# Decoder layer on one core: decay columns loaded once, one product for the sample sums, and padded rows of the matmuls' moving operand

## The chip, the cores and the metric

The kernel runs on one core of one Trainium2 chip. The metric is the device time of one execution in microseconds (us). Before the change it is 2003.5 us, the median of three runs (2000.65 to 2004.73).

## What is computed

One inference step of one decoder layer (DEPTH is 1) for two groups of requests that share the weights: 256 prompt tokens, and 8 samples of one token each. All arrays are float32, D is 2048, the feed-forward width is 5504.

```
proj = x @ w_in                      # split into q, k, v, g, a_lr(16), cb, cc, ch, mq, z_a, z_b, z_m
log_a = log_sigmoid(a_lr @ w_gla_a2 + b_gla_a2) / 16
o, s_gla = gla_recurrence(q, k, v, log_a, s_gla)       # 4 heads, state 256 x 512 a head and sample
y_a = (rms_norm(o) * silu(g)) @ w_gla_out
y_b = (cb * causal_conv3(cc * ch)) @ w_conv_out
y_m = softmax(mq @ mem_k^T / 16) @ mem_v @ w_mem_out   # prompt: mem = mem_prompt @ w_mem_k, w_mem_v; samples: caches
m = (sigmoid(z_a)*y_a + sigmoid(z_b)*y_b + sigmoid(z_m)*y_m) @ w_o
x1 = layer_norm(2**0.25 * x + m)
f = (silu(causal_conv3(x1 @ w_ffn_gate) + b) * (x1 @ w_ffn_up)) @ w_ffn_down
y = layer_norm(2**0.25 * x1 + f)
```

Besides y, the memory's keys and values of the prompt and the new states (recurrence, convolution, feed-forward convolution) are written out.

## The kernel before

Everything is held transposed: 128 channels on the partitions, and a row of NT = 264 float32 (256 prompt tokens, 8 samples) for each block of 128 channels. A row of x is thus 1056 bytes, and the tiles XH and XL (L320, L321) hold the 16 rows of x one behind the other, so that row kt begins 1056·kt bytes into the tile. Float32 precision is made out of the faster fp32r matmul: x and every weight are split into a high part (rounded to fp32r) and a low part (the rest), and for each block of weights three matmuls are summed: weights high by x high (L302), weights high by x low (L303), weights low by x high (L304). X1H and X1L (L1155, L1156) hold the output of the first norm in the same way, in the place of XH and XL.

`group` (L280) computes 512 output channels. It walks over the 16 rows of x two at a time (a granule, L260): SP loads a 512 KB block of weights into one of four staging buffers `ws`, ScalarE rounds it to `wh` and VectorE subtracts for `wl` (both on L277, three buffers each), and TensorE runs 4 x 2 x 3 = 24 matmuls of 264 columns, for each of the 4 output blocks first the even row and then the odd one. After each granule `tick` (L229) advances a clock by one and works off what is due: `later(n, f)` runs f in n ticks, and a queue holds units that load something on SP and then work on it (`put`, `pop`). `flush` (L243) empties the queue and runs all that waits. Instructions of an engine run in the order in which a scheduler has put them; that order follows the program, moved by priorities.

The order of the stages: memory queries of x (L394); keys and values of the prompt's memory (L509), with the samples' key caches read meanwhile by `key_unit` (L425: a cache block, and a row of queries from DRAM spread over the partitions, `T<-dq`); attention into the memory (L548 to L577: product L554, maximum L557, L558, exponential L561, transpose L568, second product L575); `flush` at L578; the decay's projection (L591); q, k and v; the z_m, convolution, z_b, g and z_a projections with the output projections of the branches; w_o (L1118); the first norm; gate, up and down (L1204 on); the second norm.

The places that the change touches:

- **The decay's columns** (L591): the 32 columns from A0 of w_in (16 of the decay and 16 more) are wanted three times side by side, 96 columns, for the three products with w_gla_a2 split into high and low. They are loaded three times for each of two blocks of eight rows, six loads of 128 KB, and multiplied as a group of 96 columns, 16 rows x 3 = 48 matmuls. L593 and L594 make the high and the low part of the result.
- **The sums over partitions** (`sum_rows`, L459): six times (two for the memory's values of the samples, four for the heads' states) a tile R of 128 partitions x 8 samples x 16 is summed over the 4 partitions that are equal modulo 32. Four float32 matmuls of 32 columns add up into one place (L473), each with another 128-column window of `strip`, whose block of 32 columns holds the sum of four identities; VectorE copies the result out (L474).
- **A head's own key** (L635 to L640): two float32 matmuls of 8 columns (L638), one for each half of the 256 channels.
- **The memory's keys and values** (L528): four stores of 512 KB from the POOL queue, at once when a block is done.
- **The samples' past rows of the feed-forward convolution** (L1057 to L1059): one tile `fr` of 86 partitions x 8 x 128, of the S4 buffers that the samples' state units use too, is filled by two transfers of 172 KB from the POOL queue. `turn_fpast` transposes it in two halves, 20 and 24 ticks later (L1067).
- **Small tiles**: masks, vs, cpast, clast, omS, qkb, qas, and later fpast and flast, each have a place of their own.

Of the kernel before, what the change touches and what calls it, by code (L numbers as in the profile page):

```python
# [17 lines left out]
P = 128  # L18
# [16 lines left out]
def layer_kernel(ctx, tc, x_prompt, x_sample, mem_prompt, cache_mem_k, cache_mem_v, state_gla, state_conv,  # L35
# [15 lines left out]
    def big(dt=F32, shape=(P, 4, NT)):  # L51
        return sb.tile(list(shape), dt, tag="T4", bufs=16, name=nm("T4"))
# [13 lines left out]
    def small():  # L66
        return ps.tile([P, 512], F32, tag="sm", bufs=3, name=nm("sm"))
# [46 lines left out]
    smask = sb.tile([P, NP], F32, name="smask")  # L114
    masks = sb.tile([P, len(LEVELS) + 1, P], I8, name="masks")
    upper = masks[:, len(LEVELS)]
    strip = sb.tile([P, 7 * 32], F32, name="strip")
    vcol = sb.tile([P, NV], F32, name="vcol")
    fcol = sb.tile([P, 172], F32, name="fcol")

    quads = lambda c: strip[:, 96 - 32 * c:224 - 32 * c]
# [121 lines left out]
    def flush():  # L243
        while queue:
            pop()
        while waiting:
            due(True)
# [174 lines left out]
    pS = sb.tile([P, 2, 32], F32, tag="qs", name="pS")  # L422
    omS = sb.tile([P, 8, NS], F32, name="omS")

# [34 lines left out]
    def sum_rows(sums, b, z, dst, after=None):  # L459


        if b == 0:
            sums[0] = t2(F32, (P, NS, 16))
        zt = t2(F32, (P, 512))
        V.transpose(zt, z)
        R = sums[0]
        V.tensor_reduce(R[:, b], zt.rearrange("p (c j) -> p c j", j=32), AX.X, ALU.add)

        def product():
            pt = small()  # L470
            o = pt[:, 0:4 * NS].rearrange("p (b j) -> p b j", b=NS)
            for c in range(4):
                T.matmul(o, quads(c), R.rearrange("p b (j c) -> p b j c", c=4)[:, :, :, c], start=(c == 0), stop=(c == 3))  # L473
            V.tensor_copy(dst() if callable(dst) else dst, pt[:, 0:4 * NS].rearrange("p (b j) -> p j b", b=NS))  # L474
            if after:
                after()

        if b == NS - 1:
            later(3, product)
# [29 lines left out]
    for name, w, dst in (("k", w_mem_k[0], o_mk), ("v", w_mem_v[0], o_mv)):  # L509
# [18 lines left out]
        for m in range(2):  # L528
            G.dma_start(dst[0, 0, m * P:(m + 1) * P].rearrange("m h d -> m (h d)"), mt_[m])
        mtok[name] = mt_  # L530
# [17 lines left out]
    for c in range(2):  # L548
# [21 lines left out]
        for hh in range(2):  # L570
            for d in range(2):
# [13 lines left out]

    wr = big(F32, (96, 1024))
    wa2 = big(F32R, (96, 1024))
    G.memset(wr, 0.0)
    for i in range(3):
        G.dma_start(wr[32 * i:32 * i + 16], w_gla_a2[0])  # L590
# [7 lines left out]
    eas = sb.tile([P, H, 2, NS], F32, name="eas")  # L598
    vs = sb.tile([P, 4, H, NS], F32, name="vs")
# [3 lines left out]
    qkb = sb.tile([P, H, NS], F32, name="qkb")  # L603
    qas = sb.tile([P, H, 2, NS], F32, name="qas")

# [5 lines left out]
    def head(h, q, k, vf):  # L611
# [16 lines left out]
        def decays_of_samples():  # L628

            S.activation(eas[:, h], la[:, :, NP:NT], AF.Exp, scale=1.0 / 16.0)  # L630
            dot = tiny((P, 2, NS))
            V.tensor_mul(dot, qks[:, 0, h], qks[:, 1, h])
            later(1, lambda: (V.tensor_mul(qas[:, h], qks[:, 0, h], eas[:, h]), own_key(dot)))

        def own_key(dot):  # L635
            pz = small()
            for kt in range(2):
                T.matmul(pz[:, 0:NS], onesm, dot[:, kt], start=(kt == 0), stop=(kt == 1))  # L638
# [306 lines left out]

    cpast = sb.tile([P, 16, 8], F32, name="cpast")
    clast = sb.tile([P, 10, 8], F32, name="clast")
    cr = t2(F32, (P, P))
# [117 lines left out]

    later(20, lambda: turn_fpast(0))  # L1067
    later(24, lambda: turn_fpast(4))

# [332 lines left out]
```

## Time and profile before

| | |
|---|---|
| median of 3 runs | 2003.5 us (2000.65 to 2004.73) |
| the profiled execution | 2005.06 us |
| its span, first to last instruction | 2003.3 us |
| mean granted TensorE clock | 0.996 of full speed |
| TensorE busy | 1984.9 us (99%), 15,721 matmul records |
| VectorE, ScalarE, POOL busy | 1296.7, 986.3, 164.1 us |
| moved by DMA | 439 MB, 219 GB/s |

Each matmul record of the trace lasts longer than the distance to the next, since matmuls are pipelined: a record of 264 columns shows about 285 ns, and the next one begins about 122 ns after it. So busy time hides how fast TensorE goes; what counts is the distance from start to start. A float32 matmul appears as two records, an fp32r one as one. `[6.28 <-ACT wh L277]` behind a line is the idle time of that engine just before it and what is taken to have ended it.

### The profile page before, as it was taken

To read this page: it belongs to the slowest core of one execution; us is meant where nothing else is said; L and a number is where in the kernel's file an instruction comes from. 1 tells how busy PE (TensorE), PEld (TensorE's weight loads), DVE (VectorE), ACT (ScalarE), POOL (GpSimd) and SP (SyncE) were. 2 spreads that over 40 slices of the span, in tenths; PEclk is the share of its full clock that TensorE was granted. 3 is DMA by queue.
4 is the path that set the end of the run, shared out by engine and by line. 5 is a ranking of instruction groups with operands and counts; after the bars stand their busy time and mean duration, and the time that the engine had idled before them with its cause. 6 is when DMAs were issued, how large, how long until landed. Compare 5 with 4: busy or idle time off the path is not lost.

```text
span 2003.3 us, 38161 instructions
## 1 busy us (share of the span) xinstructions
PE 1984.9 (99%) x15721; PEld 1950.6 (97%) x15721; DVE 1296.7 (65%) x1947; ACT 986.3 (49%) x1348; POOL 164.1 (8%) x240
## 2 busy tenths in 40 slices
PE   9998999999999999999999999999999999999998
PEld 9887999999999999999999998999999999999997
DVE  5675866566676867865444787666665556666655
ACT  4433654454554555554444346555554445555533
POOL 4000030021310211100000201000000000000100
PEclk9999999999999999999999999999999999999999
DMA  8895866566666667866555567877777787777753
GB/s 282 272 316 189 274 201 198 176 211 197 189 190 195 201 190 241 259 173 183 179 179 181 178 213 252 256 236 231 233 246 249 259 254 238 232 233 247 237 177 119
DMA packets 235199, 439.00 MB, mean 219 GB/s; under 512 B 22862, under 2 KB 29571, under 8 KB 234889
## 3 DMA queue, kind: packets, MB, share of 16 engines
q1 hardware_dynamic: 229120, 426.86, 68.9%
q0 software_dynamic: 5040, 8.79, 1.3%
q8 instruction: 123, 2.02, 0.4%
q10 hardware_dynamic: 864, 0.92, 0.1%
q14 instruction: 52, 0.42, 0.1%
HBM read 409.76 MB, written 26.90 MB: 218 GB/s over the span
## 4 chain that ended last, share of the span: by engine, by line
PE 72%; DVE 1%; ACT 0%; issue 0%; DVEq 0%; ACTq 0%
PE mm L303 23%; PE mm L302 23%; PE mm L304 23%; PE sm L803 1%; PE sm L679 0%; PE sm L781 0%; DVE G L935 0%; PE sm L473 0%; PE sm L1276 0%; DVE wl L277 0%; PE sm L849 0%; PE sm L783 0%; PE bank L1331 0%; PE mm L1139 0%; ACT wh L277 0%
## 5 line engine op out<-in xcount | busy, mean ns | idle before, releaser
L277 DVE TENSOR_TENSOR wl<-ws,wh 128x1024 fp32r<-128x1024 f32 (+2 forms) x651 | 802.6, 1234 | 582.0 <-ACT wh L277 580.2
L277 ACT CAST wh<-ws 128x1024 fp32r<-128x1024 f32 (+2 forms) x651 | 676.1, 1039 | 878.0 <-PE mm L303 770.0
L302 PE MATMUL mm<-XH,wh 128*128 128x264 f32 (+1 forms) x2064 | 592.8, 287 | 1.8 <-ACT wh L277 1.0
L303 PE MATMUL mm<-XL,wh 128*128 128x264 f32 (+1 forms) x2064 | 588.8, 286 | 0.0
L304 PE MATMUL mm<-XH,wl 128*128 128x264 f32 (+1 forms) x2064 | 586.2, 285 | 0.7 <-DVE wl L277 0.7
L302 PE MATMUL mm<-T,wh 128*128 128x264 f32 x1456 | 415.1, 285 | 0.0
L303 PE MATMUL mm<-T,wh 128*128 128x264 f32 x1456 | 414.2, 284 | 0.0
L304 PE MATMUL mm<-T,wl 128*128 128x264 f32 x1456 | 413.8, 284 | 0.0
L302 PEld LDWEIGHTS mm<-XH,wh 128*128 128x128 f32 (+1 forms) x2064 | 390.0, 189 | 2.7 <-ACT wh L277 1.2
L302 PE MATMUL mm<-X1H,wh 128*128 128x264 f32 x1376 | 391.5, 284 | 0.0
L303 PE MATMUL mm<-X1L,wh 128*128 128x264 f32 x1376 | 391.1, 284 | 0.0
L304 PE MATMUL mm<-X1H,wl 128*128 128x264 f32 x1376 | 391.0, 284 | 0.0
L303 PEld LDWEIGHTS mm<-XL,wh 128*128 128x128 f32 (+1 forms) x2064 | 389.4, 189 | 0.5 <-DVE XL L317 0.2
L304 PEld LDWEIGHTS mm<-XH,wl 128*128 128x128 f32 (+1 forms) x2064 | 387.8, 188 | 1.2 <-DVE wl L277 1.0
L302 PEld LDWEIGHTS mm<-T,wh 128*128 128x128 f32 x1456 | 274.1, 188 | 0.1
L303 PEld LDWEIGHTS mm<-T,wh 128*128 128x128 f32 x1456 | 274.0, 188 | 0.1
L304 PEld LDWEIGHTS mm<-T,wl 128*128 128x128 f32 x1456 | 273.8, 188 | 0.0
L302 PEld LDWEIGHTS mm<-X1H,wh 128*128 128x128 f32 x1376 | 259.4, 189 | 0.2 <-issue 0.2
L303 PEld LDWEIGHTS mm<-X1L,wh 128*128 128x128 f32 x1376 | 259.0, 188 | 0.2 <-DVE T L1160 0.2
L304 PEld LDWEIGHTS mm<-X1H,wl 128*128 128x128 f32 x1376 | 258.4, 188 | 0.0
L1080 POOL DMA_DIRECT2D out_dram<-S x2 | 1.1, 551 | 637.2 <-DVE S L1077 637.2
L521 PE MATMUL mm<-wl,T 128*128 128x512 f32 x128 | 50.6, 395 | 0.0
(363 smaller groups left out, 1485.7 us busy)
## 6 DMA issues: line engine op xcount, KB each, us to landing
ws<-in_w_in_dram SPq DMA_DIRECT2D x255, 512.0 KB, 4.0
ws<-in_w_ffn_down_dram SPq DMA_DIRECT2D x84, 512.0 KB, 4.8
ws<-in_w_ffn_gate_dram SPq DMA_DIRECT2D x80, 512.0 KB, 4.4
ws<-in_w_ffn_up_dram SPq DMA_DIRECT2D x80, 512.0 KB, 4.7
S<-in_state_gla_dram SPq DMA_DIRECT2D x64, 512.0 KB, 5.3
ws<-in_w_gla_out_dram SPq DMA_DIRECT2D x32, 512.0 KB, 3.7
ws<-in_w_o_dram SPq DMA_DIRECT2D x32, 512.0 KB, 4.2
out_dram<-S SPq DMA_DIRECT2D x32, 512.0 KB, 4.2
```

The costliest lines, as they stand in the source:

```text
L277: split_at[:] = [S.copy(wh, st).ins, V.tensor_sub(wl, st, wh.bitcast(F32)).ins]
L302: T.matmul(p, wh[:, t, cs], xh(kt), start=(kt == 0), stop=False)
L303: T.matmul(p, wh[:, t, cs], xl(kt), start=False, stop=False)
L304: i = T.matmul(p, wl[:, t, cs], xh(kt), start=False, stop=(kt == nk - 1))
L521: T.matmul(pts[m], a, wl[:, t], start=False, stop=False)
L803: T.matmul(pt, kd[:, st, kt * P:(kt + 1) * P], vt[:, st], start=(st == 0), stop=(st == 1))
L1080: G.dma_start(o_pffn[0, 0, u].rearrange("(k f) -> k f", f=P), rows[:, 0])
```

## The change

The decay's 32 columns are loaded once for each block of eight rows. ScalarE spreads them into three copies of the high part, VectorE puts the low part beside them, which makes 128 weight columns; two matmuls a row (all 128 columns by x high, 96 by x low) take the place of three, and the low products come out in a fourth block of 32 partitions, which a fourth copy of w_gla_a2 takes in.

The sums over partitions become one float32 matmul of 128 columns with `modulo` (four identities of 32 added, four times side by side), whose result is copied out in four pieces of 32 partitions, by VectorE and ScalarE in turn. A head's own key adds its two halves on VectorE first and needs one matmul.

Rows of XH, XL, X1H and X1L are 288 elements apart instead of 264, 1152 bytes, of which 264 are used. The room comes from one tile `part`: masks, vs, cpast, clast, omS, qkb and qas lie in `early`, and fpast and flast in `late`, which takes the same place after it.

The stores of the memory's keys and values are put 2 and 8 ticks later, and the queue alone is emptied behind the attention, not all that waits. The feed-forward past is loaded on SP, two pieces of 43 rows for each sample and one sample a tick, and turned 14 and 18 ticks later.

```diff
-    masks = sb.tile([P, len(LEVELS) + 1, P], I8, name="masks")
+    early = sb.tile([P, 1150], F32, tag="part", name="early")
+    masks = early[:, 0:256].bitcast(I8).rearrange("p (l t) -> p l t", t=P)
+    vs = early[:, 256:384].rearrange("p (j h b) -> p j h b", j=4, h=H)
+    cpast = early[:, 384:512].rearrange("p (b k) -> p b k", k=8)
+    clast = early[:, 512:592].rearrange("p (t j) -> p t j", j=8)
+    omS = early[:, 592:656].rearrange("p (d b) -> p d b", b=NS)
+    qkb = early[:, 656:688].rearrange("p (h b) -> p h b", b=NS)
+    qas = early[:, 688:752].rearrange("p (h k b) -> p h k b", h=H, k=2)
...
-        G.memset(strip, 0.0)
-        for a in range(4):
-            G.tensor_tensor(strip[:, 96:128], strip[:, 96:128], ident[:, 32 * a:32 * a + 32], ALU.add)
+        i4 = ident.rearrange("p (a i) -> p a i", a=4)
+        V.tensor_add(modulo[:, 0:2], i4[:, 0:2], i4[:, 2:4])
+        V.tensor_add(modulo[:, 3], modulo[:, 0], modulo[:, 1])
+        V.tensor_copy(modulo[:, 0:3], modulo[:, 3:4].to_broadcast([P, 3, 32]))
...
-    XH = sb.tile([P, 16, NT], F32R, tag="XH", name="XH")
-    XL = sb.tile([P, 16, NT], F32R, tag="XL", name="XL")
+    XH = sb.tile([P, 16, 288], F32R, tag="XH", name="XH")[:, :, 0:NT]
+    XL = sb.tile([P, 16, 288], F32R, tag="XL", name="XL")[:, :, 0:NT]
...
             pt = small()
-            o = pt[:, 0:4 * NS].rearrange("p (b j) -> p b j", b=NS)
+            T.matmul(pt[:, 0:P], modulo.rearrange("p a i -> p (a i)"), R.rearrange("p b c -> p (b c)"),
+                     start=True, stop=True)
+            d = dst() if callable(dst) else dst
             for c in range(4):
-                T.matmul(o, quads(c), R.rearrange("p b (j c) -> p b j c", c=4)[:, :, :, c], start=(c == 0), stop=(c == 3))
-            V.tensor_copy(dst() if callable(dst) else dst, pt[:, 0:4 * NS].rearrange("p (b j) -> p j b", b=NS))
+                own = pt[32 * c:32 * c + 32, 0:P].rearrange("p (b j c) -> p j b c", b=NS, c=4)[:, :, :, c]
+                (S.copy if c % 2 else V.tensor_copy)(d[32 * c:32 * c + 32], own)
...
-            G.dma_start(dst[0, 0, m * P:(m + 1) * P].rearrange("m h d -> m (h d)"), mt_[m])
+            later(2 + 6 * m, lambda dst=dst, mt_=mt_, m=m: G.dma_start(
+                dst[0, 0, m * P:(m + 1) * P].rearrange("m h d -> m (h d)"), mt_[m]))
...
-    flush()
+    while queue:
+        pop()
...
-    for i in range(3):
+    for i in range(4):
         G.dma_start(wr[32 * i:32 * i + 16], w_gla_a2[0])
-    pa, = group([(win, A0, 32)] * 3, 16, xh, xl, gk=8)
-    aT = sb.tile([96, NT], F32R, name="aT")
-    S.copy(aT, pa[0:96])
+    pa = ps.tile([P, 512], F32, tag="mm", bufs=5, name=nm("mm"))[:, :NT]
+    for g in (0, 8):
+        lead[0] += 1
+        with tc.high_priority(offset=700):
+            st = sb.tile([P, 8, 32], F32, tag="ws", bufs=4, name=nm("ws"))
+            staged[:] = [nc.sync.dma_start(
+                st, win[g * P:(g + 8) * P, A0:A0 + 32].rearrange("(k p) c -> p k c", p=P)).ins]
+        with tc.high_priority(offset=450):
+            wa = sb.tile([P, 8, P], F32R, tag="wh", bufs=3, name=nm("wh"))
+            split_at[:] = [S.copy(wa[:, :, 0:96].rearrange("p k (a c) -> p k a c", a=3),
+                                  st.unsqueeze(2).to_broadcast([P, 8, 3, 32])).ins,
+                           V.tensor_sub(wa[:, :, 96:P], st, wa[:, :, 0:32].bitcast(F32)).ins]
+        for t in range(8):
+            kt = g + t
+            if kt:
+                T.matmul(pa[0:96], wa[:, t, 0:96], xl(kt), start=False, stop=False)
+            i = T.matmul(pa, wa[:, t], xh(kt), start=(kt == 0), stop=(kt == 15))
+            if kt == 0:
+                T.matmul(pa[0:96], wa[:, t, 0:96], xl(kt), start=False, stop=False)
+        last_mm[:] = [i.ins]
+        tick(1 - g // 8, 2)
+    aT = sb.tile([P, NT], F32R, name="aT")
+    S.copy(aT, pa)
...
+            V.tensor_add(dot[:, 0], dot[:, 0], dot[:, 1])
...
-            for kt in range(2):
-                T.matmul(pz[:, 0:NS], onesm, dot[:, kt], start=(kt == 0), stop=(kt == 1))
+            T.matmul(pz[:, 0:NS], onesm, dot[:, 0], start=True, stop=True)
...
-    fpast = sb.tile([P, 16, NF], F32, name="fpast")
-    flast = sb.tile([P, 10, NF], F32, name="flast")
+    late = sb.tile([P, 26, NF], F32, tag="part", name="late")
+    fpast, flast = late[:, 0:16], late[:, 16:26]
     fr = s4((2 * NF, NS, P))
-    for u in range(2):
-        G.dma_start(fr[u * NF:(u + 1) * NF], state_ffn_conv[0, :, u].rearrange("b (k f) -> k b f", f=P))
+    def load_fpast(b):
+        with tc.issue_after(staged[0]):
+            for u in range(2):
+                nc.sync.dma_start(fr[u * NF:(u + 1) * NF, b], state_ffn_conv[0, b, u].rearrange("(k f) -> k f", f=P))
+    for b in range(NS):
+        later(1 + b, lambda b=b: load_fpast(b))
...
-    later(20, lambda: turn_fpast(0))
-    later(24, lambda: turn_fpast(4))
+    later(14, lambda: turn_fpast(0))
+    later(18, lambda: turn_fpast(4))
...
-    X1H = sb.tile([P, 16, NT], F32R, tag="XH", name="X1H")
-    X1L = sb.tile([P, 16, NT], F32R, tag="XL", name="X1L")
+    X1H = sb.tile([P, 16, 288], F32R, tag="XH", name="X1H")[:, :, 0:NT]
+    X1L = sb.tile([P, 16, 288], F32R, tag="XL", name="X1L")[:, :, 0:NT]
```

More of the change, by code (lines that the diff above doesn't have):

```diff
@@ L114, in layer_kernel @@
     smask = sb.tile([P, NP], F32, name="smask")
-    masks = sb.tile([P, len(LEVELS) + 1, P], I8, name="masks")
+    early = sb.tile([P, 1150], F32, tag="part", name="early")
[6 more added lines that the diff above has]
+    qas = early[:, 688:752].rearrange("p (h k b) -> p h k b", h=H, k=2)
     upper = masks[:, len(LEVELS)]
-    strip = sb.tile([P, 7 * 32], F32, name="strip")
+    modulo = sb.tile([P, 4, 32], F32, name="modulo")
     vcol = sb.tile([P, NV], F32, name="vcol")
     fcol = sb.tile([P, 172], F32, name="fcol")
-    quads = lambda c: strip[:, 96 - 32 * c:224 - 32 * c]
     def constants():
-        G.memset(strip, 0.0)
-        for a in range(4):
-            G.tensor_tensor(strip[:, 96:128], strip[:, 96:128], ident[:, 32 * a:32 * a + 32], ALU.add)
+        i4 = ident.rearrange("p (a i) -> p a i", a=4)
+        V.tensor_add(modulo[:, 0:2], i4[:, 0:2], i4[:, 2:4])
+        V.tensor_add(modulo[:, 3], modulo[:, 0], modulo[:, 1])
+        V.tensor_copy(modulo[:, 0:3], modulo[:, 3:4].to_broadcast([P, 3, 32]))
         vrow = t2(F32, (NV, P))
@@ L422, in layer_kernel @@
     pS = sb.tile([P, 2, 32], F32, tag="qs", name="pS")
-    omS = sb.tile([P, 8, NS], F32, name="omS")
     def key_unit(b, c):
@@ L602, in layer_kernel @@
     o_tiles = {}
-    qkb = sb.tile([P, H, NS], F32, name="qkb")
-    qas = sb.tile([P, H, 2, NS], F32, name="qas")
     def o_head(h):
```

7 lines of the change are left out of this document (2 added, 5 removed).

## The prediction

> **What bounds the kernel now.** I read the page's first and fourth part, then the groups by line, then the waits, then the timeline wherever TensorE sat idle.
>
> ```profile
> span 2003.3 us, 38161 instructions
> PE 1984.9 (99%) x15721; PEld 1950.6 (97%) x15721; DVE 1296.7 (65%) x1947; ACT 986.3 (49%) x1348; POOL 164.1 (8%) x240
> ...
> PE 72%; DVE 1%; ACT 0%; issue 0%; DVEq 0%; ACTq 0%
> ...
> ACT wh L277 <- PE mm L303: 770.0, 469, 4.2
> ```
>
> TensorE is the bound from end to end: 99% busy, and the chain that ended last is its own. ScalarE, which prepares the next weights, spends 770 us waiting until a buffer has been used up by TensorE, 1.6 us each time: weights are ahead of the matmuls, as a rule. So only three things can shorten the run: fewer matmuls, a shorter distance between matmuls, and the few places where TensorE stands still or runs at half clock. The change has something of each.
>
> ```profile
> L302 PE MATMUL mm<-XH,wh 128*128 128x264 f32 (+1 forms) x2064 | 592.8, 287 | 1.8 <-ACT wh L277 1.0 <-DVE G L985 0.7
> L302 PE MATMUL mm<-X1H,wh 128*128 128x264 f32 x1376 | 391.5, 284 | 0.0
> L473 PE MATMUL sm<-T,strip 128*128 128x32 f32 x48 | 5.9, 274 | 0.0
> L638 PE MATMUL sm<-ty,onesm 128*128 128x8 f32 x16 | 2.0, 235 | 0.0
> ```
>
> In these groups the counts matter. Matmuls that read rows of x or of the first norm's output are 3 x (2064 + 1376) = 10,320 (L302, L303 and L304 have the same counts). The decay's are 48 of them, three for each of 16 rows.
>
> **Part 1, the rows.** Where nothing else interferes, in a gate group, the timeline gives the start of every 24th matmul; each stretch is one granule of the same 24 matmuls, on rows 0 and 1, 2 and 3, 4 and 5, 6 and 7.
>
> ```profile
> 1371.61 0.28 PE L302 MATMUL mm<-X1H,wh 128*128 128x264 f32 x1
> ...
> 1374.51 0.29 PE L302 MATMUL mm<-X1H,wh 128*128 128x264 f32 x1
> ...
> 1377.45 0.28 PE L302 MATMUL mm<-X1H,wh 128*128 128x264 f32 x1
> ...
> 1380.37 0.28 PE L302 MATMUL mm<-X1H,wh 128*128 128x264 f32 x1
> ...
> 1383.29 0.28 PE L302 MATMUL mm<-X1H,wh 128*128 128x264 f32 x1
> ```
>
> 2.90, 2.94, 2.92, 2.92 us: together 11.68 us for 96 matmuls, 121.7 ns each. The granules differ in nothing but the rows that they read (the weight blocks always lie 512 bytes apart), and rows begin 1056·kt bytes into the tile, which is 32·kt modulo 256. So the distance does depend, a little, on where a row begins: rows 0 and 1 cost 120.8 ns a matmul, rows 2 and 3 122.5. With 1152 bytes every row begins at 0 or 128 modulo 256, where rows 0 and 4 begin now. Row 0 is in the shortest granule, row 4 in a middling one. The ends: nothing at all, if the pair and not the row makes it; and twice the 0.8 ns by which the first granule lies under the mean, if row 0 alone makes its granule short, 1.7 x 10,320 = 17 us. A loss is bounded by the longest granule, 0.8 ns above the mean, 8.6 us. I take the nearest row, the first granule, 0.83 ns x 10,320 = 8.6 us, less a fifth because row 4's granule is no shorter than the mean: 7 us.
>
> The Trainium skill, "TensorE: Matmul & The Clock Gate", section "Back-to-back issue gap", gives the distance between matmuls, loads of weights apart, as the columns over 2.4 GHz and 2.5 ns more, 112.5 ns for 264 columns by an estimate from it, without a term for the address; by it this part would bring nothing, and the sum would be 7 us less. The trace disagrees in the size (121.7 ns) and in the constancy (2.90 to 2.94 us).
>
> **Part 2, fewer matmuls.** The decay goes from 48 to 32 matmuls at 121.7 ns: 2.0 us, all on TensorE's path. For the sums and the own key the price of a float32 record is read from a run of eight in the timeline (the last line is one of the waits, with its total, number and longest):
>
> ```profile
> 880.32 0.98 PE L473 MATMUL sm<-T,strip 128*128 128x32 f32 x8
> 881.14 0.37 PE L302 MATMUL mm<-XH,wh 128*128 128x264 f32 x1
> ...
> DVE T L474 <- PE sm L473: 5.0, 4, 2.6
> ```
>
> Eight records (four matmuls) push the next work back by 0.82 us, 0.10 a record. One matmul remains of four, six records less, six times: 36; the own key saves two, four times: 8. That is 44 x 0.10 = 4.4 us. The remaining matmul has 128 columns instead of 32; I cost that at nothing, and if the columns bound it at twice the record's price it takes back 1.2 us. The copy in four pieces instead of one, half of it now on ScalarE, lies under ScalarE's 1.6 us of spare time per granule; without that cover it is four short copies, six times. ScalarE newly waits for the product there, with the next cast of weights queued behind it and TensorE waiting for that cast; VectorE's copy has waited there so far, 2.6 us at the longest, less than one granule, and three are buffered.
>
> **Part 3, the first standstill, at 161 us.** It is the one large hole:
>
> ```profile
> 160.69 0.28 PE L302 MATMUL mm<-XH,wh 128*128 128x264 f32 x1
> 163.57 0.42 DVE L439 SCALAR_TENSOR_TENSOR T<-S,T 128x256 f32<-128x256 f32 x1 [6.18 <-DMA T<-dq]
> ...
> 165.16 0.47 ACT L561 ACTIVATE T<-sm,ty 128x256 f32<-128x256 f32 x1 [6.24 <-DVE ty L558]
> ...
> 167.25 0.45 PE L568 MATMUL sm<-ident,T 128*128 128x128 f32 x1 [6.28 <-ACT wh L277]
> ```
>
> Read upwards: TensorE's transposes of the softmax wait for the exponential, that for the maximum's scaling on VectorE, and VectorE stands 6.18 us in a key unit that waits for its row of queries, `T<-dq`. What is late is a transfer. Its cause is in the queues; the lines are SP's and POOL's timeline, the busy time by stretch, and the DMA issues:
>
> ```profile
> 142.59 5.72 SPq L270 DMA_DIRECT2D ws<-in_w_in_dram  x4
> ...
> 152.81 0.46 SPq L430 DMA_DIRECT2D T<-dq  x1
> ...
> 154.19 0.53 POOL L529 DMA_DIRECT2D out_dram<-T  x1 [0.40 <-ACT T L527]
> ...
> 154.72 0.97 POOL L588 MEMSET T<- 96x1024 f32 x1
> ...
> 155.98 1.45 POOL L590 DMA_DIRECT2D T<-in_w_gla_a_dram  x3 [0.29 <-POOL T L588]
> ...
> 135.00:140.00 5.00, 5.00 (x23) 4.10 (x22) 3.50 (x9) 1.52 (x3) 0.00 (x0) 1.00 1.01 377
> 140.00:145.00 5.00, 5.00 (x23) 4.11 (x23) 2.90 (x6) 1.66 (x2) 0.00 (x0) 1.00 0.87 191
> 145.00:150.00 5.00, 5.00 (x24) 4.11 (x23) 3.47 (x10) 1.89 (x2) 0.00 (x0) 1.00 0.82 145
> ...
> 166.10:172.90 6.80, 5.66 (x19) 4.97 (x20) 3.87 (x7) 1.28 (x3) 0.00 (x0) 0.50 0.78 245
> ...
> ws<-in_w_in_dram SPq DMA_DIRECT2D x6, 128.0 KB, 5.9
> ```
>
> (The last three columns of a stretch are the granted clock, the DMA engines' share and GB/s.) The DMA engines are full here, but while the six loads of the decay's columns run they move 168 GB/s in 8.45 us of engine time where the stretch before moved 373 GB/s at the same share: 1.68 MB would have taken 4.5 us, so the six cost 3.9 us more than their bytes. Four of them go: 2.6 us of that, and their 0.5 MB, 1.4 us more, in all 4.0. The two stores of the memory's values, 1 MB, were issued on POOL up to 154.19 us; now they stand behind POOL's memset (0.97 us) and four small loads (1.45 us for three), some 2.5 us later, so part of them falls behind the late transfer: an estimate of 1.5 us. (POOL has nothing else to do there, so the 2 and 8 ticks alter its order, not its time by themselves.) The transfer then lands 5.5 us earlier, at about 158. VectorE's work from there to the transposes takes 167.25 - 163.57 = 3.7 us, so they start at about 161.7; TensorE, which ends its decay group 2.0 us earlier, at 159.0, waits 2.7 us instead of 6.3: 3.6 us saved, 0 if the transfer is as late as now, 6.3 if the order is mended altogether.
>
> Behind the hole the clock is 0.50 for 6.8 us, with 5.66 us of work in it: 2.8 us lost. Whether it stays depends on the rest of the hole. The other place with half clock (below) had 1.7 us of idle time in two pieces and then 3.5 us at half clock, so a dip behind 2.7 us is possible; I count 2.4 of the 2.8 and so 6.0 us for this part, with 0 and 9.1 as ends. The Trainium skill, same page, section "Part 1: The HAM clock gate", has the clock halved after an idle window of about 3.4 us; by that a remainder of 2.7 us would leave it whole, and the part would be 6.4. The trace disagrees: 1.7 us were enough.
>
> **Part 4, the second standstill, at 874 us.**
>
> ```profile
> 874.75 0.39 PE L302 MATMUL mm<-XH,wh 128*128 128x264 f32 x1 [0.98 <-ACT wh L277]
> ...
> 876.01 0.59 PE L304 MATMUL mm<-XH,wl 128*128 128x264 f32 x1 [0.75 <-DVE wl L277]
> ...
> 876.00:879.50 3.50, 3.49 (x16) 3.49 (x17) 2.51 (x3) 1.24 (x2) 0.00 (x0) 0.51 0.70 176
> ...
> ws<-in_w_in_dram SPq DMA_DIRECT2D x255, 512.0 KB, 4.0
> ...
> S<-in_state_ffn_conv_dram POOLq DMA_DIRECT2D x2, 172.0 KB, 19.5
> ...
> ws<-in_w_in_dram SPq DMA_DIRECT2D x11, 512.0 KB, 8.2
> ```
>
> Weights land late here: 8.2 us in the stretch from 845 to 880 against 4.0 in the whole run. In that stretch lie the two transfers of the feed-forward past, 19.5 us each. They leave, and with them 1.73 us of idle time and half of 3.5 us: 3.4 us. What is paid elsewhere:
>
> ```profile
> L965 SPq DMA_DIRECT2D out_dram<-T x8: 293/300/361, 695.4 to 703.2; - x8
> ...
> ws<-in_w_o_dram SPq DMA_DIRECT2D x32, 512.0 KB, 4.2
> ```
>
> sixteen small transfers on SP, two a tick. The nearest, small stores of a state, hold SP 0.30 us each, 0.6 us a tick, while SP has one load of weights to issue in a granule of 2.92 us. Four staging buffers are 11.7 us of matmuls; a load needs 4.2: 7.5 us of slack. So nothing, unless they are slow like the two before.
>
> **Part 5, at nothing.** `late` waits for the last reader of `early`; that is the last head's own token, 305 us before fpast is first written:
>
> ```profile
> 875.88 0.18 DVE L824 TENSOR_TENSOR ty<-vs,qkb 128x32 f32<-128x32 f32 x1
> ...
> L1065 ACT COPY fpast<-sm x2: 436/437/438, 1181.0 to 1193.2; 128x344 f32<-128x344 f32 x2
> ```
>
> `modulo` is formed on VectorE in the first stage, where it is half idle. The padded rows are read by POOL and written by VectorE and ScalarE in the same number of elements.
>
> **The sum.** 7.0 + 2.0 + 4.4 + 6.0 + 3.4 = 22.8 us. The span of 2003.3 becomes 1980.5, the profiled execution of 2005.06 us 1982.3; the median of the runs is 1.6 us under that execution, so 1981 us.
>
> **Rivals.**
> - *The padding does nothing*: the four granules together decide, some limit common to all rows holds the mean at 121.7 ns, and the differences only shift work from one granule to the next. For it: the differences are under 1%, and the sum over four granules is even. Against it: 24 matmuls are long for a mere shift. 1988 us. The Trainium skill's rule on the gap, above, is on this side.
> - *The first hole stays*: VectorE gets the row of queries earlier, but the softmax chain of 3.7 us, or another transfer in the same full queue, becomes the last. For it: the DMA engines' share is about 1 on both sides of the decay's loads. Then 6.0 us are missing: 1987 us. Both rivals together: 1994.
> - *Slower*: the sixteen loads on SP are as harmful as the two on POOL were, each pair delaying the weights behind it in SP's own queue by more than the 7.5 us of slack. Then each of eight ticks costs what the second standstill costs, 3.4 us: 27 us, and 2008. It decides from about 2.9 us a tick on. Against it: 43 rows a piece instead of 344.
>
> **How the numbers follow.** Forecast, within 7 us of 1981: 0.52. Padding alone fails 0.18, the hole alone stays 0.15, both 0.06 (1994), SP's loads harm a little or a lot 0.06 (1999 to 2010), better than forecast 0.03. A range from 1971 (17 us from the rows) to 1996 leaves out about 0.1 on the slow side and less on the other. A change under 0.2%, 4 us, can't be told from none. Only the cases with harmful loads come near that: faster 0.93, same 0.04, slower 0.03.
>
> **What would show it.** Granules of gate and up at 2.90 us or less, all alike, prove part 1; still 11.68 us for four disproves it. TensorE's idle time before L568 near 161 us under 3 us; no half clock near 876; no idle time in w_o between 1090 and 1215 us; 60 matmul records fewer (16, 36 and 8). The prediction is wrong if weights wait for DMA in w_o, or if the rows' granules become uneven in a new way.

## The result, and the profile after

The changed kernel takes 1988.91 us, the median of five runs (1987.13 to 1989.45). The kernel before, on the same chip, takes 2001.75 (2000.65 to 2004.73, five runs). The ratio is 0.9929, with a 95% interval of 0.9916 to 0.9943: faster by 12.8 us. The forecast was 1981 us, from a sum of 22.8 us. The time lies inside the stated range of 1971 to 1996, but outside the 7 us on either side of 1981, and where the rival "the padding does nothing" stood, at 1988.

The profiled execution of the changed kernel took 1989.18 us. These are its page's span, its busy times and the chain that ended last (PE is TensorE, PEld its loading of weights, DVE VectorE, ACT ScalarE; in other views SPq is SP's queue):

```profile
span 1987.5 us, 38068 instructions
...
PE 1976.2 (99%) x15661; PEld 1941.1 (98%) x15661; DVE 1297.5 (65%) x1960; ACT 987.3 (50%) x1360; POOL 158.1 (8%) x234
...
PE 72%; DVE 1%; ACT 0%; issue 0%; DVEq 0%
```

TensorE is still the bound, with 60 matmul records fewer, as counted. The two spans differ by 15.8 us, the medians by 12.8: the execution of the kernel before that was profiled, 2005.06 us, was slower than all five. To see where the time went, each group of matmuls in the order of the program was matched in the two traces, and the difference of their first starts taken. A positive step is time saved. The table has the large steps and the places where a gain was forecast; elsewhere the difference moves up and down by 0.4 us at most and loses 0.5 us in all:

| stage | step in us | forecast |
|---|---|---|
| from the first group to the decay's first matmul (memory's queries, keys and values) | -1.7 | 0 |
| the decay's matmuls, from their first to q's first | 2.0 | 2.0 |
| from q's first matmul to the first group of k (first standstill, half clock) | 8.6 | 6.0 |
| at five of the six sums over partitions | 0.66, 0.52, 0.72, 0.71, 0.59 | 0.6 each |
| a head's own key, four times | 0.0 | 0.8 |
| the g projection (second standstill and the sixth sum) | 4.4 | 3.4 and 0.6 |
| gate and up, all groups together (1376 x 3 = 4128 of the 10,320 matmuls on padded rows) | 0.0 | 2.8 of the rows' 7.0 |

Over each of the two long runs of gate and up groups the difference moves by 0.04 us at most. The timeline of the changed kernel shows how. These are the starts of five granules of one gate group:

```profile
1355.69 0.29 PE L309 MATMUL mm<-X1H,wh 128*128 128x264 f32 x1
...
1358.61 0.29 PE L309 MATMUL mm<-X1H,wh 128*128 128x264 f32 x1
...
1361.53 0.29 PE L309 MATMUL mm<-X1H,wh 128*128 128x264 f32 x1
...
1364.45 0.29 PE L309 MATMUL mm<-X1H,wh 128*128 128x264 f32 x1
...
1367.37 0.29 PE L309 MATMUL mm<-X1H,wh 128*128 128x264 f32 x1
```

2.92 us four times, where there were 2.90, 2.94, 2.92 and 2.92. The granules are alike now, as forecast, but at the mean of the old ones and not at the shortest: 11.68 us for four, before and after.

At the first standstill the timeline of VectorE, POOL and TensorE answers to the rows shown of before (L445, L578, L538 and L600 were L439, L568, L529 and L588):

```profile
153.50 0.42 DVE L445 SCALAR_TENSOR_TENSOR T<-S,T 128x256 f32<-128x256 f32 x1 [2.67 <-DMA T<-dq]
...
156.20 1.05 POOL L538 DMA_DIRECT2D out_dram<-T  x2 [47.19 <-DVE T L536]
157.25 0.97 POOL L600 MEMSET T<- 128x1024 f32 x1
158.51 1.94 POOL L602 DMA_DIRECT2D T<-in_w_gla_a_dram  x4 [0.29 <-POOL T L600]
...
162.51 0.63 PE L578 MATMUL sm<-ident,T 128*128 128x128 f32 x4 [0.20 <-DVE T L574]
```

VectorE still waits for its row of queries, 2.67 us, but is released at 153.50 instead of 163.57, 10.1 us earlier; the transposes wait 0.20 us instead of 6.28, and the granted clock is 1.00 until the kernel's last 9 us. And SP's timeline, where the six small loads had stood:

```profile
140.69 0.37 SPq L608 DMA_DIRECT2D ws<-in_w_in_dram  x1
...
143.50 0.37 SPq L608 DMA_DIRECT2D ws<-in_w_in_dram  x1
...
147.66 0.47 SPq L436 DMA_DIRECT2D T<-dq  x1
```

The row's transfer is issued at 147.66 us instead of 152.81.

The 1.7 us that are lost ahead of the decay have the same form, at an earlier row of queries. In the changed kernel's timelines of VectorE and TensorE:

```profile
119.35 0.43 DVE L445 SCALAR_TENSOR_TENSOR T<-S,T 128x256 f32<-128x256 f32 x1 [4.09 <-DMA T<-dq]
...
121.67 0.50 PE L530 MATMUL mm<-wl,T 128*128 128x512 f32 x1 [0.95 <-DVE wl L284]
```

VectorE waits 4.09 us for that row, the low part of the weights, which it works on next, comes late, and TensorE stands still for 0.95 us. In the kernel before, VectorE waited 1.65 us for the same row and TensorE not at all. Two of the seven further versions of the changed kernel below show such a standstill too (1.21 us with four matmuls for a sum, 0.83 us with the stores at once). What makes it, and where the rest of the 1.7 us goes, is open.

### The profile page after: what moved, and what is told of

It is laid out like the page before. It is cut to its first block, busy times and chain, and to the rows that moved or that the text cites. A ratio compares the mean times of both kernels' runs of the same rounds, so it can differ in the third digit from the quotient of the medians.

```text
span 1987.5 us, 38068 instructions
## 1 busy us (share of the span) xinstructions
PE 1976.2 (99%) x15661; PEld 1941.1 (98%) x15661; DVE 1297.5 (65%) x1960; ACT 987.3 (50%) x1360; POOL 158.1 (8%) x234
## 4 chain that ended last, share of the span: by engine, by line
PE 72%; DVE 1%; ACT 0%; issue 0%; DVEq 0%
PE mm L309 23%; PE mm L310 23%; PE mm L311 23%; PE sm L832 1%; PE sm L708 0%; DVE wl L284 0%; PE sm L810 0%; DVE G L964 0%; PE sm L1309 0%; PE bank L1364 0%; PE sm L878 0%; PE sm L812 0%; DVE YT L1370 0%; ACT L655 0%; DVE G L1012 0%
## 5 line engine op out<-in xcount | busy, mean ns | idle before, releaser
L309 PE MATMUL mm<-XH,wh 128*128 128x264 f32 x2048 | 587.5, 287 | 0.7 <-DVE G L1012 0.5
L310 PE MATMUL mm<-XL,wh 128*128 128x264 f32 x2048 | 583.1, 285 | 0.0
L311 PE MATMUL mm<-XH,wl 128*128 128x264 f32 x2048 | 579.8, 284 | 0.0
L310 PE MATMUL mm<-T,wh 128*128 128x264 f32 x1456 | 414.6, 285 | 0.0
L311 PE MATMUL mm<-T,wl 128*128 128x264 f32 x1456 | 414.2, 284 | 0.0
L310 PE MATMUL mm<-X1L,wh 128*128 128x264 f32 x1376 | 391.2, 284 | 0.0
L311 PE MATMUL mm<-X1H,wl 128*128 128x264 f32 x1376 | 390.4, 284 | 0.0
L309 PEld LDWEIGHTS mm<-XH,wh 128*128 128x128 f32 x2048 | 385.2, 188 | 1.3 <-DVE G L1012 0.7
L310 PEld LDWEIGHTS mm<-XL,wh 128*128 128x128 f32 x2048 | 385.2, 188 | 0.5
L311 PEld LDWEIGHTS mm<-XH,wl 128*128 128x128 f32 x2048 | 384.4, 188 | 0.2
L310 PEld LDWEIGHTS mm<-T,wh 128*128 128x128 f32 x1456 | 274.2, 188 | 0.1
L311 PEld LDWEIGHTS mm<-T,wl 128*128 128x128 f32 x1456 | 274.0, 188 | 0.0
L310 PEld LDWEIGHTS mm<-X1L,wh 128*128 128x128 f32 x1376 | 258.5, 188 | 0.2 <-DVE T L1193 0.2
L311 PEld LDWEIGHTS mm<-X1H,wl 128*128 128x128 f32 x1376 | 258.6, 188 | 0.0
```

What stands on the lines that cost most here:

```text
L309: T.matmul(p, wh[:, t, cs], xh(kt), start=(kt == 0), stop=False)
L310: T.matmul(p, wh[:, t, cs], xl(kt), start=False, stop=False)
L311: i = T.matmul(p, wl[:, t, cs], xh(kt), start=False, stop=(kt == nk - 1))
```

## The experiments

Three questions: why the rows gave nothing, what makes and ends the first standstill, and what the second one was. "Runs of the kernel before" are those on the same chip as the experiment; their median lay between 2001.3 and 2002.5 us.

### The rows

**The changed kernel with rows 1056 bytes apart again.**

```diff
-    XH = sb.tile([P, 16, 288], F32R, tag="XH", name="XH")[:, :, 0:NT]
+    XH = sb.tile([P, 16, NT], F32R, tag="XH", name="XH")
```

(and so for XL, X1H and X1L)

> The changed kernel with rows 264 elements (1056 bytes) apart again, nothing else undone. Theory 'even pace': the mean distance between matmuls on these rows is 121.7 ns wherever they begin, padding only evens it out; then the time is that of the changed kernel, 1988.9 us within 2, and the granules go back to 2.90, 2.94, 2.92, 2.92 us, 11.68 us for four. Theory 'row gain eaten': padded rows do save about 7 us, and something else in the change costs as much; then this kernel is about 7 us slower, 1996 us.

Measured: 1987.11 us, ratio 0.9927 (0.9914 to 0.9941), the same as the changed kernel's 0.9929. Its timeline shows the uneven granules again:

```profile
1307.89 0.28 PE L309 MATMUL mm<-X1H,wh 128*128 128x264 f32 x1
...
1310.80 0.29 PE L309 MATMUL mm<-X1H,wh 128*128 128x264 f32 x1
...
1313.74 0.28 PE L309 MATMUL mm<-X1H,wh 128*128 128x264 f32 x1
...
1316.65 0.28 PE L309 MATMUL mm<-X1H,wh 128*128 128x264 f32 x1
...
1319.57 0.28 PE L309 MATMUL mm<-X1H,wh 128*128 128x264 f32 x1
```

2.91, 2.94, 2.91, 2.92: 11.68 us once more. The address moves a start by some hundredths within the four granules and takes them back.

**The kernel before with the padded rows and the shared tile alone.**

```diff
-    masks = sb.tile([P, len(LEVELS) + 1, P], I8, name="masks")
+    early = sb.tile([P, 1150], F32, tag="part", name="early")
+    masks = early[:, 0:256].bitcast(I8).rearrange("p (l t) -> p l t", t=P)
...
-    XH = sb.tile([P, 16, NT], F32R, tag="XH", name="XH")
+    XH = sb.tile([P, 16, 288], F32R, tag="XH", name="XH")[:, :, 0:NT]
```

> The kernel before with nothing but the rows 1152 bytes apart and the small tiles in the shared place that makes room for them. Even pace: the time of the kernel before, 2001.8 us within 2, with all granules of a gate group at 2.92 us. If the padding gains by itself and is eaten by another part of the change: about 7 us less, 1995 us.

Measured: 2002.31 us, ratio 0.9998 (0.9989 to 1.0007, eleven runs). Padding alone is worth nothing, from this side too.

**The changed kernel with the low part of x in 256 columns instead of 264.** It leaves out the low part of the eight samples.

```diff
-                        T.matmul(p, wh[:, t, cs], xl(kt), start=False, stop=False)
+                        T.matmul(p[:, 0:NP], wh[:, t, cs], xl(kt)[:, 0:NP], start=False, stop=False)
```

> The changed kernel, but the matmul of the weights' high part with the low part of x (the second of each three) reads 256 columns instead of 264: the samples' low part is left out of the computation. 4880 matmuls get 8 columns shorter. If the distance is set by the columns streamed (121.7 ns for 264), each loses 8/264 of it, 3.7 ns, or 3.3 ns if a fixed part stays: 16 to 18 us less, about 1972 us. If a limit other than columns sets the pace (loads of weights, issue), nothing: 1989 us. Even pace says that the granules stay alike; 'row gain eaten' has no view on it.

Measured: 1966.77 us, ratio 0.9827 (0.9814 to 0.984), 20.3 us under the kernel with rows of 1056 bytes on the same chip. Two starts from its timeline, 27 sets of three matmuls apart:

```profile
1340.06 0.28 PE L309 MATMUL mm<-X1H,wh 128*128 128x264 f32 x1
...
1349.81 0.29 PE L309 MATMUL mm<-X1H,wh 128*128 128x264 f32 x1
```

9.75 / 27 = 361.1 ns for three, where the changed kernel has 11.68 / 32 = 365.0: eight columns fewer in one matmul of three save 3.9 ns, 0.49 ns a column, and 4880 such matmuls 19 us of the 20.3, a little more than the 16 to 18 us expected. The distance between matmuls follows the columns, not the address. This is a price and no version of the kernel.

### The first standstill

**The changed kernel with the decay's columns loaded three times**, 48 matmuls and six loads again.

```diff
-    pa = ps.tile([P, 512], F32, tag="mm", bufs=5, name=nm("mm"))[:, :NT]
-    for g in (0, 8):
...
+    pa, = group([(win, A0, 32)] * 3, 16, xh, xl, gk=8)
```

> The changed kernel with the decay's columns loaded three times and multiplied as 48 matmuls again; stores of the memory's keys and values stay where the change put them. If the six loads make the row of queries late, the hole near 161 us comes back: 2 us of matmuls and up to 9 us of idle time and half clock, 1996 to 2000 us. If the stores made it, only the 16 matmuls come back: 1991 us.

Measured: 1992.53 us, ratio 0.9962 (0.995 to 0.9974) and 5.4 us over the kernel with rows of 1056 bytes on the same chip. The five executions fall into two groups, three from 1991.84 to 1992.53 and two at 1996.54 and 1997.45; the median thus lies under the range expected of the loads and over the time expected of the stores. The profiled one, 1997.45, has the hole whole. From its timelines of SP, VectorE and TensorE, and a stretch of its busy times with the granted clock behind them:

```profile
138.22 2.63 SPq L277 DMA_DIRECT2D ws<-in_w_in_dram  x3
...
141.76 6.10 SPq L277 DMA_DIRECT2D ws<-in_w_in_dram  x4
...
152.14 0.46 SPq L436 DMA_DIRECT2D T<-dq  x1
...
162.92 0.42 DVE L445 SCALAR_TENSOR_TENSOR T<-S,T 128x256 f32<-128x256 f32 x1 [6.17 <-DMA T<-dq]
...
166.60 1.09 PE L578 MATMUL sm<-ident,T 128*128 128x128 f32 x4 [6.31 <-ACT wh L284]
...
162.50:172.70 10.20, 6.10 (x21) 5.41 (x22) 6.60 (x17) 2.34 (x7) 0.00 (x0) 0.50 0.85 280
```

So the six loads bring the hole back with everything else of the change in place, but how much of it shows in the time differs from one execution to the next. The three shorter executions lie 10 us under the kernel before, of which the sums and the second standstill explain about 4 (3.0 and 0.8 us by the runs below); what shortens the hole in them is open, since none of them was profiled. Seven issues of weights (the six, and one of 512 KB) hold SP for 8.7 us, and the row of queries, behind them in SP's order, is issued at 152.14 as in the kernel before.

**The kernel before with the decay's columns loaded once, and nothing else.**

```diff
-    pa, = group([(win, A0, 32)] * 3, 16, xh, xl, gk=8)
+    pa = ps.tile([P, 512], F32, tag="mm", bufs=5, name=nm("mm"))[:, :NT]
+    for g in (0, 8):
...
```

> The kernel before with one part of the change: the decay's columns loaded once (two loads of weights instead of six) and 32 matmuls instead of 48. Theory 'six loads hold SP': the two matmul groups saved give 2.0 us, the idle time near 161 us (6.3 to 6.5 us in the kernel before) and its half clock (about 3 us) go: 9 to 11 us faster, 1991.5 to 1993.5, and the query row's last transfer is issued by SP about 5 us earlier than in the kernel before. Rival 'the hole needs the whole change' (the stores moved back, the sums and the spare rows as well): only the 2.0 us and part of the hole, 2 to 5 us faster, 1997 to 2000.

Measured: 1991.59 us, ratio 0.9948 (0.9936 to 0.9961): 9.7 us of the whole change's 12.8, as the first theory had it. SP issues the row at 144.87 us. Both standstills from its TensorE timeline:

```profile
159.77 0.63 PE L568 MATMUL sm<-ident,T 128*128 128x128 f32 x4 [0.24 <-DVE T L564]
...
863.62 0.39 PE L304 MATMUL mm<-XH,wl 128*128 128x264 f32 x1 [0.74 <-DVE wl L277]
```

The first is gone, the second still there. The rest of the change is not needed for the first.

**Six loads, but four of them issued by POOL.** The same bytes in the same pieces, and the same 48 matmuls, as two experiments above.

```diff
-                    staged[:] = [nc.sync.dma_start(st[:, :, o:o + c], a.rearrange("(k p) c -> p k c", p=P)).ins]
+                    i = (nc.gpsimd if o and ncols == 96 else nc.sync).dma_start(
+                        st[:, :, o:o + c], a.rearrange("(k p) c -> p k c", p=P)).ins
+                    if not (o and ncols == 96):
+                        staged[:] = [i]
```

> The changed kernel with the decay's columns loaded three times again and 48 matmuls, as in the run that did so, but four of the six loads are issued by POOL and not by SP: the same bytes in the same small pieces, the same matmuls. Theory 'SP's queue is held by slow issues': the query row is issued as early as in the changed kernel, the hole before the softmax's transposes is under 1 us, and the time is the changed kernel's and 2.0 us: 1989.5 to 1991. Rival 'the bytes and pieces fill the DMA engines': the row lands as late as with all six on SP, the hole is 4 to 6.5 us with a dip of the clock behind it: 1992.5 to 1997.5.

Measured: 1989.08 us, ratio 0.9937 (0.9924 to 0.9951), five executions within 2.1 us. The timelines of POOL, SP, VectorE and TensorE (L448 and L581 are L445 and L578 here):

```profile
138.69 1.81 POOL L277 DMA_DIRECT2D ws<-in_w_in_dram  x2 [30.73 <-DVE wl L287]
141.51 1.75 POOL L277 DMA_DIRECT2D ws<-in_w_in_dram  x2 [1.01 <-DVE wl L287]
...
145.31 0.81 SPq L439 DMA_DIRECT2D T<-dq  x1
...
151.43 0.42 DVE L448 SCALAR_TENSOR_TENSOR T<-S,T 128x256 f32<-128x256 f32 x1 [1.73 <-DMA T<-dq]
...
158.94 0.63 PE L581 MATMUL sm<-ident,T 128*128 128x128 f32 x4 [0.52 <-ACT wh L287]
```

This separates the two readings of the standstill. With all the bytes of the six loads still moved, the row is issued 6.8 us earlier than with six on SP, and TensorE waits 0.52 us instead of 6.31. The stretch from 145 to 150 us, first with six on SP, then with four of them on POOL (the last two columns are the DMA engines' share and GB/s):

```profile
145.00:150.00 5.00, 5.00 (x23) 4.04 (x22) 3.53 (x10) 1.29 (x3) 0.00 (x0) 1.00 0.72 129
...
145.00:150.00 5.00, 5.00 (x23) 4.06 (x22) 3.57 (x10) 1.36 (x2) 0.00 (x0) 1.00 1.02 314
```

With six on SP the DMA engines are busy for 0.72 of this time and move 129 GB/s, with four on POOL 1.02 and 314. What made the row's issue late was its place behind loads that SP took long to issue, and not the DMA engines' load. Why SP took long over them is not shown. The Trainium skill, "Perfetto Trace Analysis", section "DMA Optimizations", says that spreading transfers over several issuing engines may help when an issuing engine is busy writing out descriptors and the data movement is not the limit; the trace agrees (8.7 us of SP, against 3.6 us of an otherwise idle POOL).

**The changed kernel with the memory's stores at once.**

```diff
-            later(2 + 6 * m, lambda dst=dst, mt_=mt_, m=m: G.dma_start(
-                dst[0, 0, m * P:(m + 1) * P].rearrange("m h d -> m (h d)"), mt_[m]))
+            G.dma_start(dst[0, 0, m * P:(m + 1) * P].rearrange("m h d -> m (h d)"), mt_[m])
...
-    while queue:
-        pop()
+    flush()
```

> The changed kernel with the stores of the memory's keys and values issued at once and everything that waits worked off behind the attention, as before; the decay's columns stay loaded once. If the stores made the hole near 161 us, part of it comes back: 3 to 6 us more, 1992 to 1995 us. If the decay's loads did, nothing: 1989 us within 2.

Measured: 1987.34 us, ratio 0.9927 (0.9914 to 0.9939). This part of the change is worth nothing, and it hardly moves the stores: POOL issues the two that lie near the hole at 155.48 and 156.29 us here, at 156.20 and 156.72 in the changed kernel, in both after a wait of over 46 us for their data. What stores that really came later would do isn't tested.

### The second standstill

**The changed kernel with the feed-forward past on POOL again**, two transfers.

```diff
-    for b in range(NS):
-        later(1 + b, lambda b=b: load_fpast(b))
+    for u in range(2):
+        G.dma_start(fr[u * NF:(u + 1) * NF], state_ffn_conv[0, :, u].rearrange("b (k f) -> k b f", f=P))
```

> The changed kernel with the feed-forward past loaded by two transfers from the POOL queue again, turned 20 and 24 ticks later, as before. If these transfers made the weights late near 860 us, the standstill near 870 us and its half clock come back: 3.4 to 3.8 us more, 1992.5 us. If the standstill had another cause (the decay's loads or the sums moved the work around it), it stays away and the time is 1989 us.

Measured: 1987.25 us, ratio 0.9929 (0.9917 to 0.9942): no slower, and no idle time of TensorE. But the waits of ScalarE and the DMA issues between 825 and 880 us show that weights were late again (their loads took 5.1 us to land in this stretch of the kernel before):

```profile
ACT wh L284 <- DMA ws<-in_w_in_dram: 6.4, 4, 2.8
...
ws<-in_w_in_dram SPq DMA_DIRECT2D x19, 512.0 KB, 7.1
S<-in_state_ffn_conv_dram POOLq DMA_DIRECT2D x2, 172.0 KB, 17.1
```

In the changed kernel ScalarE never waits for weights in this stretch. So the expected return of the standstill did not come; the buffers held out.

**The kernel before, profiled once more**, to see how fixed its standstills are.

> The kernel before once more, for a second profiled execution. The one read for the prediction took 2005.1 us, the median is 2001.8. If the two standstills and the half clock behind them differ from execution to execution, this profile shows a shorter one or a missing dip, 1.7 to 3 us less; if they are fixed, the difference lies elsewhere.

Measured: 2002.39 us, span 2000.6. The first standstill is there as it was (6.48 us at 166.6, then 6.8 us at half clock). The second one, in TensorE's timeline, ScalarE's waits between 825 and 880 us and the busy times:

```profile
873.22 0.40 PE L302 MATMUL mm<-XH,wh 128*128 128x264 f32 x1 [0.27 <-ACT wh L277]
...
874.48 0.39 PE L304 MATMUL mm<-XH,wl 128*128 128x264 f32 x1 [0.75 <-DVE wl L277]
...
ACT wh L277 <- DMA ws<-in_w_in_dram: 9.1, 5, 3.7
...
872.00:880.00 8.00, 6.98 (x55) 6.55 (x55) 5.38 (x8) 5.28 (x5) 0.00 (x0) 1.00 0.64 198
```

1.0 us of idle time and the clock at 1.00, where the first profile had 1.7 us and 3.4 us at half clock. The runs with the decay loaded once and with the padding alone show it with 0.74 and 0.76 us of idle time and a clock of 1.00 behind it. The standstill is a matter of margin, and the dip stands in one of four profiles that have it.

**The kernel before with the past on SP, and nothing else.**

```diff
-    for u in range(2):
-        G.dma_start(fr[u * NF:(u + 1) * NF], state_ffn_conv[0, :, u].rearrange("b (k f) -> k b f", f=P))
+    for b in range(NS):
+        later(1 + b, lambda b=b: load_fpast(b))
```

> The kernel before with one part of the change: the feed-forward past loaded by sixteen small transfers on SP instead of two on POOL. Theory 'the two transfers make the second standstill of the kernel before': no idle time near 874 us, 1.0 us (idle time alone, without a dip of the clock) to 3.4 us faster: 1999 to 2001.5. Rival 'the transfers are not what makes it' (in the changed kernel they did not bring it back): the idle time near 874 us stays, the time within 1 us of the kernel before.

Measured: 2000.42 us, ratio 0.9991 (0.9983 to 1.0, eleven runs). Its trace has no idle time near 874 us and no wait of ScalarE for weights there; the hole at 166 us is 6.47 us. The four profiles of kernels with the old sums and the transfers on POOL have the standstill, this one without the transfers has not: they do make it in the kernel before. It is worth about 1 us by the medians, with an interval that ends at none.

### The sums

**The changed kernel with four matmuls of 32 columns for a sum, and one copy.**

```diff
-            T.matmul(pt[:, 0:P], modulo.rearrange("p a i -> p (a i)"), R.rearrange("p b c -> p (b c)"),
-                     start=True, stop=True)
...
+                T.matmul(o, quads(c), R.rearrange("p b (j c) -> p b j c", c=4)[:, :, :, c], start=(c == 0), stop=(c == 3))
```

> The changed kernel with the sums over partitions by four matmuls of 32 columns and one copy again. Six runs of eight records instead of two: 0.6 us each, 3.6 us more, 1992.5 us. If the copies on ScalarE cost something in the changed kernel, less than that.

Measured: 1990.32 us, ratio 0.994 (0.9927 to 0.9952), 3.0 us over the kernel with the stores at once, which ran on the same chip and has the changed kernel's sums; 3.6 us were expected. The intervals of the two ratios overlap, so the size of the gain rests on the steps of 0.52 to 0.72 us in the table.

## Why the prediction was right, and where not

**Part 1, the rows, 7.0 us: measured 0.** This is the step that failed. By the two profiles 15.8 us came of the 22.8 forecast, and the 7.0 us that are missing are the rows'. That the other parts add up so well is luck: 2.6 us more at the first standstill stand against the 1.7 us lost ahead of it and the 0.8 us of the own key that did not come. The prediction took the shortest granule as what every granule could be. But the four granules shared one total, and the prediction's own first rows said so: 11.68 us for 96 matmuls. The rival put it rightly (shifts from one granule to the next under a limit common to all rows). The argument against the rival, that 24 matmuls are long for a mere shift, was wrong: a shift of 0.02 to 0.04 us needs no length. The Trainium skill's rule on the gap between matmuls ("TensorE: Matmul & The Clock Gate", section "Back-to-back issue gap") has no term for the address; in that the runs agree. The formula behind the prediction's 112.5 ns is, by that section, for isolated matmuls; for a stream of weight loads and matmuls it has measured about 81 ns at 128 columns and 131 ns at 512. The 121.7 ns at 264 columns of these traces lie between the two.

**Part 2, 2.0 + 4.4 us.** The sums came out as costed: 0.6 us each. The timeline of the changed kernel shows one:

```profile
864.25 0.28 PE L311 MATMUL mm<-XH,wl 128*128 128x264 f32 x1
864.38 0.38 PE L478 MATMUL sm<-T,modulo 128*128 128x128 f32 x2
864.51 0.37 PE L309 MATMUL mm<-XH,wh 128*128 128x264 f32 x1
864.72 0.28 PE L310 MATMUL mm<-XL,wh 128*128 128x264 f32 x1
```

From L311 to L310 are 0.47 us where two distances of 0.12 would stand: the two records cost 0.23 us. Counted in the same way, the eight of the kernel before cost 0.90 us (880.20 to 881.34). A record of 128 columns costs 0.11 us like one of 32, as taken. The own key's 0.8 us did not come. The rows, first of before, then of after:

```profile
277.32 0.51 PE L638 MATMUL sm<-ty,onesm 128*128 128x8 f32 x4
277.68 1.07 PE L664 MATMUL sm<-ident,T 128*128 128x128 f32 x8
278.71 0.63 PE L672 MATMUL sm<-T,onesm 128*128 128x256 f32 x2
```

```profile
267.88 0.29 PE L667 MATMUL sm<-ty,onesm 128*128 128x8 f32 x2
268.02 1.07 PE L693 MATMUL sm<-ident,T 128*128 128x128 f32 x8
269.23 0.67 PE L701 MATMUL sm<-T,onesm 128*128 128x256 f32 x2
```

The matmul behind it follows after 0.14 us instead of 0.36, but the product behind that begins 1.21 us later instead of 1.03. The 0.22 us go back into the next step but for 0.04; what holds that step stays open. The decay's 2.0 us came in full. These are its first matmul in the kernel before, then its first and q's first in the changed kernel:

```profile
154.65 0.47 PE L302 MATMUL mm<-XH,wh 128*96 128x264 f32 x1
```

```profile
156.47 0.47 PE L619 MATMUL mm<-XH,wh 128*128 128x264 f32 x1
...
160.55 0.28 PE L309 MATMUL mm<-XH,wh 128*128 128x264 f32 x1
```

From there to q's first matmul are 6.04 us before (it begins at 160.69, in a row of the prediction) and 4.08 us after.

**Part 3, 6.0 us: right in place, too small, and wrong in its reason.** It brought 8.6 us. The prediction counted the DMA engines' time and bytes of four loads (4.0 us) and let the stores fall behind the row (1.5 us), which brought the row 5.5 us earlier and left 2.7 us of the hole. The row was there 10.1 us earlier and nothing was left. That terms with a wrong reason came this near is luck. The stores kept their place in POOL's work: they are issued at 156.20, ahead of the memset and the small loads. The bytes don't matter either, by the run with four loads on POOL; the prediction's own rows had the DMA engines' share at 0.87 and 0.82 while the six loads were issued, so they were not full. What counts is SP: issued at 147.66 instead of 152.81, the row needs 5.8 us until VectorE has it instead of 10.8. The first half is settled by that run. Why a row that is issued later also takes 5 us longer is open. The traces offer one likely reason: in the 4 us before the row, SP issued four loads of 512 KB in the kernel before (148.92 to 152.39) and two in the changed kernel (143.91 and 147.25), and two stores of 512 KB followed the row within 1.4 us there and after 8.5 us here. No run separates these.

**Part 4, 3.4 us: right for the execution that it was read from.** The step there is 3.8 us (4.4 less one sum). It isn't worth that in other executions: without the dip of the clock it is 1.0 us, and by itself the edit brought 0.8. The sixteen loads on SP cost nothing: the w_o groups keep their distances within 0.4 us, and TensorE has no idle time there. ScalarE waits once, 1.9 us, for what its view of waits puts down to one of these loads.

**Part 5** at nothing: right for the tiles and the rows, by the padding alone (0.9998).

**The parts measured apart** add up: 9.7 us (decay loaded once, with standstill and clock), 0.8 (past on SP), 3.0 (sums), nothing (rows and tiles, stores, own key), 13.5 in all, inside the interval of the whole change, 11.4 to 16.8 us of 2001.75.

## What to carry to other kernels

When equal pieces of work differ by a hundredth and their total repeats, the difference may be a mere shift between them: look at the total over the whole period before you price the shortest piece. A standstill far from a queue may be that queue's: read which engine issues the late transfer and how long the issues ahead of it hold that engine, before you count bytes; making two small loads of six, with the sixteen matmuls that this saved, was worth 9.7 us of about 13. And profile the kernel before twice before a stall of one or two microseconds becomes a term of a sum.

## What the runs showed of the hardware that was not expected

- The distance between fp32r matmuls of 264 columns, each with its own load of weights, was 121.67 ns in the mean for rows 1056 and 1152 bytes apart; only its spread within a period of four granules (2.90 to 2.94 us) went with the address. Eight columns were worth 3.9 ns.
- The price of an issue on SP isn't a property of the transfer alone. Two loads of 128 KB in rows of 128 bytes were issued in 0.37 us each; when six of them came among 512 KB loads within 10 us, seven issues took 8.7 us together, while the DMA engines' share fell to 0.72 in a stretch of 5 us.
- Dips of the granted clock lasted 3.4, 6.8 and 10.2 us. In the traces' record of the clock its changes lie whole multiples of 3.413 us apart, from the first rise to the last fall (157.01 us, 46 of them, from the rise to the first dip in the kernel before). Standstills of 6.28 us there and 6.31 us in the run with the decay loaded three times were followed by dips of 6.8 and 10.2 us, 1.7 us of idle time in two pieces by one of 3.4 us, and 1.0 us by none. The Trainium skill, "TensorE: Matmul & The Clock Gate", section "Part 1: The HAM clock gate", has the activity judged in windows of about 3.4 us that run freely; these lengths are one, two and three of them, so the trace agrees. That an idle window of the full length is needed does not fit the 1.7 us.
